# First group of the first FFN: two weight sums moved from VectorE to adding transfers, and the banked functions of every group placed one entry later

## The chip, the cores and the metric

The kernel runs on one core of a Trainium2 chip. The metric is device time in microseconds (us) for one execution, the median of several. Five engines matter here: TensorE (PE, with its weight loads shown as PEld), VectorE (DVE), ScalarE (ACT), GpSimd (POOL) and SyncE (SP). The last two, and ACT now and then, issue the transfers, which run on 16 DMA engines.

## The reference, cut to what matters

The block is one layer of a streaming encoder on 256 frames of 2048 channels, all in float32:

```
x = x + 0.5 * swiglu_ffn(rmsnorm(x, g1), w1_gate, w1_up, w1_down)      # d_ff = 5632
h = rmsnorm(x, gm); proj = h @ w_in                                    # attention, retention, gates
x = x + (sigmoid(gate_a) * branch_a + sigmoid(gate_r) * branch_r) @ w_out
x = x + 0.5 * swiglu_ffn(rmsnorm(x, g2), w2_gate, w2_up, w2_down)
out = rmsnorm(x, gf)
swiglu_ffn(x, wg, wu, wd) = (silu(x @ wg) * (x @ wu)) @ wd
```

The change lies in how `x @ wg` and `x @ wu` are computed in the two FFNs, and in the same machinery for some columns of `w_in`.

## The kernel before, in words

**Entries.** The whole program is one list of entries (`steps`). Each entry multiplies 256 rows of weights by 512 columns. Its `prep` splits the float32 weights into a high and a low part, `hi` by an ACT cast (L136) and `lo` by a DVE subtraction (L137); its `products` are three matmuls for every pair of operands (hi·hi and hi·lo at L147 and L148, lo·hi at L150). A standard entry has 12 matmuls, an entry of a group 6. Four pairs of `hi` and `lo` tiles are in use in turn.

**Order.** `run` walks over the entries. At entry c it first prepares entries up to c+3 (`prep_upto`; fewer at the start), then runs whatever was put off to c with `later(n, fn)`, which means "n entries from here", then issues the products of c. Each engine has its own queue and works through it in program order. So "one entry later" moves an instruction behind the next entry's casts and subtractions in its engine's queue, and POOL, which has little to do, may run far ahead of the others as long as nothing that it waits for is missing.

**Groups.** Two blocks of 512 columns, one of `wu` and one of `wg`, that meet the same operand make a group (`Strassen`): seven products of half the depth stand for eight. A group has 28 entries in four phases. Phase 0 uses the kept weights `k` of four blocks (entries r0 to r3) and their sums `x + k` (entries s0 to s3); phase 1 and phase 2 use freshly loaded weights (r) and further sums (s); phase 3 uses four last sums. The blocks are numbered jc = 0 to 3. Tile names in the profile follow this: in the first group `z10`, `loz1003s` is the low part for phase 0, block 3, entry s, and `z10x`, `z10k` are the two weight tiles of a block.

**First sums.** POOL issues the loads of `k` and `x` for the four blocks (L559, 512 KB each). The first sum x + k is made in one of three ways: by DVE when r of that block is prepared (L548, `first_once`), which is what happens to a block that is not in `group.added`; by an adding transfer `add_on` (L564), which POOL issues `add_wait` = 6 entries behind the load of `x`, for a block in `group.added`; or by DVE later, if nothing did it before. In an FFN the first group has no added blocks, the second has block 0, and all others have blocks 0 and 1 (`ADDED[:n]`, L732). `add_on` waits on POOL's queue until both tiles have landed.

**End of a phase.** `end` moves finished sums of products out of PSUM. Two of the four results of a group are made by DVE from two parts: `c12` (L667) and `c22` (L678), both two entries behind the end of a phase. One entry behind each follows `evict(t, 1, r)`: in an FFN an ACT Silu in place (L801), in the mixing stage an ACT Sigmoid or Silu and a transfer to DRAM (L1090, L1094), for the queries only bookkeeping. A DVE multiplication of `evict(t, 0, ...)` (L804) uses the function's result some entries later.

**Start of the kernel.** `weave` puts ten standard entries (the gate block 10 and the beginning of its partner) ahead of the first group, so that r0 of group `z10` is entry 10; then come r1, a standard entry, s0, r2, s1, r3, a standard entry, s2 and s3, which is entry 19. The first group's eight loads belong to entries 4 to 11, and wait for the third block of the transposed input (`third_block`, L851). In the same stretch ACT makes the squares of the norm (L438), ACT and DVE the sums of the activations (`add_up`, L496 to L510), and POOL the power that gives the norm's scale (L385).

The few lines in which the two edits sit:

```
later(self.add_wait, lambda: add_on(jc))            # in second(), behind the load of x
if jc not in self.added and not self.early:         # in prep of phase 0, entry r
    self.first_once(jc)
later(1, lambda: self.evict(0, 1, r))               # in c12, and likewise in c22
group.added, group.early = group.added[:n], n == 0 and ahead > 8
```

Of the kernel before, what the change touches and what calls it, by code (L numbers as in the profile page):

```python
# [41 lines left out]
RET_WAIT = (14, 5)  # L42
HELD = 6
MIX_ADDED = (0,)
MIX_AHEAD = 12
FIRST_WAIT = 4
HEAD_AT = (3, 6, 10, 13, 17, 20, 24, 27)
# [35 lines left out]
def block_kernel(ctx: ExitStack, tc: tile.TileContext, x, g1, w1g, w1u, w1d, gm, w_in, rel, woa, wor, wo,  # L83
# [21 lines left out]
    def tmp_tile(name, tag="t", bufs=None):  # L105
        return tmp.tile([P, NB], F32, tag=tag, name=name, bufs=bufs)
# [9 lines left out]
    def later(n, fn):  # L116
        due.setdefault(state["step"] + n, []).append(fn)
# [34 lines left out]
    def standard(job, k0):  # L152

        made = {}
        c = len(steps)

        parts = [slice(j, j + 1) for j in range(KC)] if c == 0 else [slice(0, KC)]

        def load():
            made["raw"] = weights_tile(f"raw{c}")  # L160
            fetch(made["raw"], job.w, job.rows[k0], job.col0, parts)

        def prep():
            if c > 0:
                made["hl"] = split(made.pop("raw"), c)
                return

            hi, lo = made["hl"] = split_tiles(c)
            raw = made.pop("raw")
            for p in parts:  # L170
                nc.vector.tensor_copy(hi[:, p, :], raw[:, p, :])
            first_low.extend(lambda p=p: nc.vector.tensor_sub(lo[:, p, :], raw[:, p, :], hi[:, p, :].bitcast(F32)) for p in parts)

        def products(only=None):
            if k0 == 0 and only in (None, 0) and not job.seed:
                open_banks(job)
            hi, lo = made["hl"]
            turns = [
                [
                    (  # L180
                        job.acc[part], job.act(k0 + j, t), (hi[:, j, cs], lo[:, j, cs]),
                        k0 + j == 0 and not job.seed, k0 + j == job.nk - 1,
                    )
                    for j in range(KC)
                ]
                for part, (t, cs) in enumerate(job.parts) if only in (None, part)
            ]

            if 0 < k0 < job.nk - KC:
                turns = [sum(turns, [])]  # L190
            for products in turns:
                three(products, bool(job.seed))
            if only is None and k0 + KC == job.nk:
                close(job)

        return Step(job, k0, load, prep, ("raw",), products)
# [329 lines left out]
    class Strassen:  # L526
# [126 lines left out]
        def end(self, phase, of_sum):  # L653

            norm, acc, wide, name = self.norm, self.acc, self.wide, self.name
            if (phase, of_sum) == (0, False):

                nc.scalar.copy(self.bank("b"), acc["a"])
            elif (phase, of_sum) == (0, True):
                wide["s5"] = tmp_tile(f"{name}s5", "scaled", 1)  # L660
                nc.scalar.activation(wide["s5"], acc["c"], AF.Copy, scale=norm.minus_scale(1))
            elif (phase, of_sum) == (1, True):
                r = tmp_tile(f"{name}c12", "qk", 4)
                nc.scalar.activation(r, acc["a"], AF.Copy, scale=norm.minus_scale(0))

                def c12():
                    nc.vector.scalar_tensor_tensor(r, acc["c"], norm.minus_scale(0), r, op0=ALU.mult, op1=ALU.add)  # L667
                    later(1, lambda: self.evict(0, 1, r))

                later(2, c12)  # L670
            elif (phase, of_sum) == (2, False):
                later(2, lambda: self.evict(0, 0, acc["b"]))
            elif (phase, of_sum) == (2, True):
                r = tmp_tile(f"{name}c22", "qk", 4)
                nc.scalar.activation(r, acc["a"], AF.Copy, scale=norm.minus_scale(1))

                def c22():
                    nc.vector.tensor_add(r, r, wide.pop("s5"))  # L678
                    later(1, lambda: self.evict(1, 1, r))

                later(2, c22)
            elif phase == 3:
                later(1, lambda: self.evict(1, 0, acc["a"]))
# [21 lines left out]
    def weave(jobs, apart, groups, lead, share, start=None, extra=0, ahead=8):  # L705


        queue = [(job, k) for job in jobs for k in range(0, job.nk, KC)]
        at_hand = {}

        def next_standard():

            if len(queue) <= apart:
                return False
            job, k = queue[0]
            if any(at_hand.get(b, len(steps) + 1) > len(steps) for b in job.needs):
                return False
            steps.append(standard(job, k))
            del queue[0]
            if job.makes is not None and k + KC == job.nk:  # L720
                at_hand[job.makes] = len(steps) + 9
            return True

        for _ in range(lead):
            next_standard()
        seconds = []
        rate = (len(queue) - apart) / (len(groups) * sum(share))
        credit = 0.0
        first = max(len(steps) - ahead, D // NB)
        for n, (b, make) in enumerate(groups.items()):  # L730
            group = make()
            group.added, group.early = group.added[:n], n == 0 and ahead > 8  # L732
            loads = group.loads()
            if start is not None and n == 0:
                loads[0] = lambda load=loads[0]: [start(), load()]
            kept.extend((first + i if n == 0 else 0, fn) for i, fn in enumerate(loads))
            for i, part in enumerate(group.steps()):
                if i == HALF_K // KC + 2:
                    seconds.append(len(steps))
                steps.extend(part)  # L740
                credit += rate * share[i]
                if i + 1 == len(share):
                    at_hand[b] = len(steps) + 7

                turn = i + 1 == 3 * (HALF_K // KC)
                if (turn or credit >= (0.2 if (i + 1) % (HALF_K // KC) == 0 else 0.6)) and next_standard():
                    credit -= 1
        if extra:
            due.setdefault(seconds[0], []).append(lambda: room.update(kept=room["kept"] + extra))
            due.setdefault(len(steps), []).append(lambda: room.update(kept=room["kept"] - extra))  # L750
        for job, k in queue:
            steps.append(standard(job, k))

    def ffn(name, norm, wg, wu, wd, after, start=None):
# [83 lines left out]
        for job, follow in zip(jobs, jobs[1:]):  # L838
            job.next = follow
        groups = {b: (lambda b=b: paired(b)) for b in range(nblocks) if b != PLAIN}  # L840
        weave(jobs, len(downs[PASSES[-1]]) * len(PASSES[-1]) * 4 // KC + HELD, groups, LEAD[start is None], SHARE, start, EXTRA)


# [94 lines left out]
    def nat_done(key, b, func, after=None):  # L938
        def done(acc):
            dst = act_tile(F32, f"{key}{b}")  # L940
            nat[key, b] = by_tokens(dst)
            for t in range(NT):
                nc.scalar.activation(nat[key, b][:, t, :], acc[t], func, scale=nm.scale(t))
            if key in to_dram:
                put_away(nat, key, b, dst)
            if after is not None:
                after()

        return done
# [125 lines left out]
    def proj(col, done, tags=("acc", "z")):  # L1075
        return Gemm(w_in0, 0, col, D // P, nm, done, tags)
# [8 lines left out]
    def gates(col1, col2, func, dsts):  # L1085
# [9 lines left out]

        return Strassen(nm, w_in0, col1, w_in0, col2, evict, MIX_ADDED)

# [6 lines left out]
    def queries():  # L1104
# [9 lines left out]

        return Strassen(nm, w_in0, QA, w_in0, QA + NB, evict, MIX_ADDED)

    groups = {"qa": queries, **groups}
    weave(
        [proj(KA + b * NB, att_qk_done("ka", b), both) for b in range(2)]
        + [proj(VA + b * NB, nat_done("va", b, AF.Copy), both) for b in range(2)]  # L1120
        + [proj(VR + b * NB, nat_done("vr", b, AF.Copy), both) for b in range(2)],
        0, groups, MIX_LEAD, MIX_SHARE, None, EXTRA, MIX_AHEAD,
    )
# [212 lines left out]
```

## Time and profile before

| what | value |
|---|---|
| runs | 2047.64, 2048.49, 2049.56 us; median 2048.49 |
| profiled execution, its own time | 2048.31 us |
| its span, first to last instruction | 2046.5 us |
| PE busy | 2031.7 us, 99% of the span |
| DVE busy | 1788.5 us, 87% |
| ACT busy | 1499.2 us, 73% |
| POOL busy | 344.8 us, 17% |
| mean granted TensorE clock | 0.999 of full speed |

The profiled execution took 1.8 us more than its span, and lies 0.18 us under the median. A matmul's recorded duration overlaps that of the next one, so PE's busy share says little about small losses; the distance between the starts of matmuls says more. The share of the other engines is an average over stages that differ.

### The profile page before, as it was taken

To read this page: it belongs to the slowest core of one execution; us is meant where nothing else is said; L and a number is where in the kernel's file an instruction comes from. 1 tells how busy PE (TensorE), PEld (TensorE's weight loads), DVE (VectorE), ACT (ScalarE), POOL (GpSimd) and SP (SyncE) were. 2 spreads that over 40 slices of the span, in tenths; PEclk is the share of its full clock that TensorE was granted. 3 is DMA by queue.
4 is the path that set the end of the run, shared out by engine and by line. 5 is a ranking of instruction groups with operands and counts; after the bars stand their busy time and mean duration, and the time that the engine had idled before them with its cause. 6 is when DMAs were issued, how large, how long until landed. Compare 5 with 4: busy or idle time off the path is not lost.

```text
span 2046.5 us, 26320 instructions
## 1 busy us (share of the span) xinstructions
PE 2031.7 (99%) x9188; PEld 1678.3 (82%) x9188; DVE 1788.5 (87%) x1837; ACT 1499.2 (73%) x1890; POOL 344.8 (17%) x403
## 2 busy tenths in 40 slices
PE   9999999999999999999999999999999999999998
PEld 7788888888888878888888888888788888888886
DVE  7999999999998799999987667569989999989996
ACT  7788887878887777777775434556788788888785
POOL 1221122212113021211120000011112221112200
PEclk9999999999999999999999999999999999999999
DMA  8888899988878689899896645576889988889973
GB/s 289 249 248 259 254 269 278 265 242 246 264 231 264 234 228 310 272 281 286 254 321 221 212 148 197 187 240 180 269 262 269 278 248 234 267 257 268 278 206 134
DMA packets 226853, 506.33 MB, mean 247 GB/s; under 512 B 15824, under 2 KB 16576, under 8 KB 226720
## 3 DMA queue, kind: packets, MB, share of 16 engines
q1 hardware_dynamic: 154560, 297.31, 43.1%
q0 software_dynamic: 67952, 198.36, 37.1%
q10 hardware_dynamic: 4208, 8.99, 1.2%
q8 instruction: 72, 1.18, 0.2%
q14 instruction: 61, 0.50, 0.1%
HBM read 472.08 MB, written 12.06 MB: 237 GB/s over the span
## 4 chain that ended last, share of the span: by engine, by line
PE 94%; DVE 2%; DMA 2%; issue 1%; ACT 0%; POOL 0%; DVEq 0%; POOLq 0%; ACTq 0%
PE acc L150 15%; PE acc L147 15%; PE acc L148 15%; DMA z1030k<-in_ffn_w_up_dram 1%; DMA z1030x<-z1030k 1%; DVE lo L137 0%; DMA raw<-in_ffn_w_gate_dram 0%; PE z704a L150 0%; PE z425a L147 0%; PE z922a L147 0%; PE z885a L148 0%; PE z226a L147 0%; PE z190a L147 0%; PE z46a L147 0%; PE z262a L148 0%
## 5 line engine op out<-in xcount | busy, mean ns | idle before, releaser
L137 DVE TENSOR_TENSOR lo<-raw,hi 128x1024 fp32r<-128x1024 f32 x351 | 428.6, 1223 | 117.7 <-ACT hi L136 116.1
L136 ACT CAST hi<-raw 128x1024 fp32r<-128x1024 f32 x351 | 367.9, 1051 | 178.7 <-PE acc L148 133.4
L824 ACT ACTIVATE xall<-acc 128x512 f32<-128x512 f32 x160 | 94.5, 590 | 13.5 <-PE acc L150 9.7
L821 ACT ACTIVATE acc<-xall 128x512 f32<-128x512 f32 x160 | 95.9, 600 | 2.5
L147 PE MATMUL acc<-hi,mgh 128*128 128x512 f32 x128 | 50.2, 392 | 0.0
L148 PE MATMUL acc<-hi,mgl 128*128 128x512 f32 x128 | 49.8, 389 | 0.0
L150 PE MATMUL acc<-lo,mgh 128*128 128x512 f32 x128 | 35.5, 389 | 0.0
L147 PE MATMUL acc<-hi,nma01h 128*128 128x512 f32 x80 | 32.5, 407 | 0.0
L147 PE MATMUL acc<-hi,nma00h 128*128 128x512 f32 x80 | 32.3, 404 | 0.0
L148 PE MATMUL acc<-hi,nma01l 128*128 128x512 f32 x80 | 31.3, 391 | 0.0
L148 PE MATMUL acc<-hi,nma00l 128*128 128x512 f32 x80 | 31.2, 390 | 0.0
L148 PE MATMUL acc<-hi,nma11l 128*128 128x512 f32 x80 | 31.2, 390 | 0.0
L147 PE MATMUL acc<-hi,nma11h 128*128 128x512 f32 x80 | 31.2, 390 | 0.0
L147 PE MATMUL acc<-hi,nma10h 128*128 128x512 f32 x80 | 31.2, 390 | 0.0
L148 PE MATMUL acc<-hi,nma10l 128*128 128x512 f32 x80 | 31.2, 390 | 0.0
L150 PEld LDWEIGHTS acc<-lo,mgh 128*128 128x128 f32 x128 | 24.0, 188 | 5.0
L148 PEld LDWEIGHTS acc<-hi,mgl 128*128 128x128 f32 x128 | 24.0, 188 | 4.9
L147 PEld LDWEIGHTS acc<-hi,mgh 128*128 128x128 f32 x128 | 24.0, 188 | 4.9
L147 PE MATMUL acc<-hi,atth 128*128 128x512 f32 x64 | 26.2, 410 | 0.0
L147 PE MATMUL acc<-hi,reth 128*128 128x512 f32 x64 | 25.3, 395 | 0.0
L148 PE MATMUL acc<-hi,attl 128*128 128x512 f32 x64 | 25.1, 392 | 0.0
L148 PE MATMUL acc<-hi,retl 128*128 128x512 f32 x64 | 24.9, 389 | 0.0
(6884 smaller groups left out, 7265.9 us busy)
## 6 DMA issues: line engine op xcount, KB each, us to landing
raw<-in_ffn_w_down_dram SPq DMA_DIRECT2D x176, 512.0 KB, 6.8
raw<-in_w_in_dram SPq DMA_DIRECT2D x80, 512.0 KB, 5.2
raw<-in_w_out_dram SPq DMA_DIRECT2D x32, 512.0 KB, 3.7
raw<-in_ffn_w_up_dram SPq DMA_DIRECT2D x16, 512.0 KB, 4.6
raw<-in_w_out_att_dram SPq DMA_DIRECT2D x16, 512.0 KB, 4.2
raw<-in_w_out_ret_dram SPq DMA_DIRECT2D x16, 512.0 KB, 3.8
raw<-in_ffn_w_gate_dram SPq DMA_DIRECT2D x15, 512.0 KB, 4.0
z390x<-in_w_in_dram POOLq DMA_DIRECT2D x8, 512.0 KB, 9.9
```

The costliest lines, as they stand in the source:

```text
L136: nc.scalar.copy(hi, raw)
L137: nc.vector.tensor_sub(lo, raw, hi.bitcast(F32))
L147: nc.tensor.matmul(acc, ahi, whi, start=first, stop=False, **more)
L148: nc.tensor.matmul(acc, alo, whi, start=False, stop=False, **more)
L150: nc.tensor.matmul(acc, ahi, wlo, start=False, stop=last, **more)
L821: nc.scalar.activation(acc, xs[t][:, cols], AF.Copy, scale=2.0)
L824: nc.scalar.activation(xs[t][:, cols], acc, AF.Copy, scale=0.5)
```

## The change

In the first FFN alone, the first group's blocks 2 and 3 get their first sum by an adding transfer, issued two entries behind the load of `x`. In all groups of both FFNs and of the mixing stage, the function of a summed bank comes two entries behind the sum, where it came one entry behind.

```
+FIRST_ADDED = (2, 3)
...
                 def c12():
                     nc.vector.scalar_tensor_tensor(r, acc["c"], norm.minus_scale(0), r, op0=ALU.mult, op1=ALU.add)
-                    later(1, lambda: self.evict(0, 1, r))
+                    later(2, lambda: self.evict(0, 1, r))
...
                 def c22():
                     nc.vector.tensor_add(r, r, wide.pop("s5"))
-                    later(1, lambda: self.evict(1, 1, r))
+                    later(2, lambda: self.evict(1, 1, r))
...
             group = make()
-            group.added, group.early = group.added[:n], n == 0 and ahead > 8
+            group.added = FIRST_ADDED if n == 0 and start is not None else group.added[:n]
+            if n == 0 and start is not None:
+                group.add_wait = 2
+            group.early = n == 0 and ahead > 8
```

`start` is given for the first FFN only.

## The prediction

> **What bounds the kernel now.** I read the page's busy times first, then the windows of the first stretches, then PE's waits there, then the chain.
>
> ```profile
> span 2046.5 us, 26320 instructions
> PE 2031.7 (99%) x9188; PEld 1678.3 (82%) x9188; DVE 1788.5 (87%) x1837; ACT 1499.2 (73%) x1890; POOL 344.8 (17%) x403
> ```
>
> PE is the bound of the kernel as a whole, so a change on DVE or ACT can only win where PE stands still. The windows tell where DVE is as full as PE:
>
> ```profile
> 20.00:40.00 20.00, 19.79 (x91) 16.10 (x90) 16.24 (x19) 16.32 (x28) 6.26 (x9) 1.00 1.01 364
> 40.00:60.00 20.00, 19.15 (x84) 15.32 (x83) 19.97 (x26) 17.35 (x30) 1.09 (x1) 1.00 0.31 93
> 60.00:80.00 20.00, 19.39 (x85) 15.37 (x84) 20.00 (x19) 14.04 (x16) 4.78 (x6) 1.00 0.88 241
> 80.00:100.00 20.00, 19.43 (x86) 14.74 (x86) 19.50 (x21) 14.57 (x19) 8.40 (x11) 1.00 1.04 301
> 100.00:120.00 20.00, 20.00 (x94) 16.66 (x93) 18.27 (x18) 16.82 (x23) 0.93 (x1) 1.00 0.83 275
> ```
>
> After the length come PE, PEld, DVE, ACT and POOL. From 40 to 100 us DVE is full (19.97, 20.00, 19.50 of 20) and PE is not; from 100 us on PE is full and DVE has room. What PE waits for between 40 and 106 us is this, and it is all DVE's:
>
> ```profile
> PE z10c L150 <- DVE loz1003s L137: 0.9, 1, 0.9
> PE acc L150 <- DVE lo L137: 0.6, 1, 0.6
> PE z10b L150 <- DVE loz1023r L137: 0.5, 1, 0.5
> ```
>
> The chain of that stretch, followed back from 106 us, says the same in order of time:
>
> ```profile
> 46.11 0.97 DVE loz1001s L137
> ...
> 49.42 1.14 DVE z10x L548
> ...
> 73.74 1.15 DVE lo L137
> ...
> 74.93 0.73 PE acc L150 x2
> ...
> 88.27 1.14 DVE loz1023r L137
> ...
> 89.44 0.44 ACT hiz1022s L136
> ...
> 89.90 1.24 DVE loz1022s L137
> ...
> 91.18 0.74 PE z10a L150 x2
> ```
>
> From 46 to 75 us the chain is on DVE without a break, and one of the two sums that the change takes away stands in it. How much PE loses is seen from the starts of its matmuls:
>
> ```profile
> 45.90 0.39 PE L147 MATMUL z10a<-hiz1002r,n1a00h 128*128 128x512 f32 x1
> 75.50 0.39 PE L147 MATMUL acc<-hi,n1a11h 128*128 128x512 f32 x1
> 93.15 0.39 PE L147 MATMUL acc<-hi,f1a10h 128*128 128x512 f32 x1
> 104.03 0.39 PE L147 MATMUL z46a<-hiz4600r,n1a00h 128*128 128x512 f32 x1
> 106.75 0.39 PE L147 MATMUL acc<-hi,f1a10h 128*128 128x512 f32 x1
> ```
>
> Between the last two lie two entries of six matmuls: 2.72 us, 0.2267 us each, the pace without waits. Between the first two lie eleven entries of the group with 66 matmuls and four and a half standard ones with 54, 120 in all, so 27.20 us at that pace, and they took 29.60: PE loses 2.40 us there. From 75.50 to 93.15 lie half a standard entry and ten of the group, 66 matmuls or 14.96 us, and eight transposes:
>
> ```profile
> 110.84 1.03 PE L394 MATMUL f1a0p<-id_sb,z10c 128*128 128x128 f32 x8
> 111.63 0.48 PE L147 MATMUL z46a<-hiz4602r,n1a00h 128*128 128x512 f32 x1
> ```
>
> Eight of them without a wait take 0.79 us, so 15.75 us of the 17.65 are work and 1.90 are lost. All that the start of the first group can give back is 2.40 + 1.90 = 4.30 us, 0.21% of the kernel. What a measurement of this kernel can tell from no change is about 0.2%, or 4.1 us.
>
> **The two sums.** Each DVE sum that goes occupies DVE's queue for 1.14 us (the chain's row at 49.42), so DVE's queue is shorter by 1.14 us from block 2's sum on and by 2.28 us from block 3's on, since in 40 to 80 us DVE is never idle for long. An earlier DVE helps only if its inputs are there. The two casts on ACT that read the sums, the wait that goes with the second, and the subtraction on DVE behind it:
>
> ```profile
> 48.66 1.05 ACT L136 CAST hiz1002s<-z10x 128x1024 fp32r<-128x1024 f32 x1
> 50.65 1.05 ACT L136 CAST hiz1003s<-z10x 128x1024 fp32r<-128x1024 f32 x1 [0.33 <-DVE z10x L548]
> ...
> 54.82 1.22 DVE L137 TENSOR_TENSOR loz1003s<-z10x,hiz1003s 128x1024 fp32r<-128x1024 f32 x1
> ```
>
> With DVE 2.28 us ahead, `loz1003s` would start at about 52.5, and its cast ends at 51.7 or, without the 0.33 us of waiting, at 51.4: the input is there. So the low part is ready at 53.8, where PE has waited for it from 55.1 (0.9 us up to its end at 56.0): that wait is gone. Followed through, ACT moves up too where it waited for DVE or PE, and I find no DVE subtraction up to `loz1023r` whose cast would then be late by more than a tenth. The second loss, at 74.93, is cut by DVE's 2.28 us as long as PE can use them, and PE's own limit is the 2.40 us above. I take 2.28.
>
> What is late next: the adding transfers themselves. POOL's queue, the landing of the loads of `x` for blocks 2 and 3 (issued at 24.08 and 25.52), and the transfers of this kind that the trace shows:
>
> ```profile
> 24.08 0.74 POOL L559 DMA_DIRECT2D z10x<-in_ffn_w_gate_dram  x1
> ...
> 25.52 0.74 POOL L559 DMA_DIRECT2D z10x<-in_ffn_w_gate_dram  x1
> 53.80 1.09 POOL L385 TENSOR_TENSOR n1rstd<-v,mhalf 128x2 f32<-128x2 f32 x1 [27.54 <-DVE v L384]
> ```
>
> ```profile
> z10x<-in_ffn_w_gate_dram POOLq DMA_DIRECT2D x1, 512.0 KB, 13.0
> ```
>
> ```profile
> z10x<-in_ffn_w_gate_dram POOLq DMA_DIRECT2D x1, 512.0 KB, 15.5
> ```
>
> ```profile
> DMA to landing us min/median/max: 4.6/6.7/12.2
> ```
>
> The loads land at 37.1 and 41.0 us. POOL waits for each in its queue, and behind the two added issues stands nothing until the power at 53.80, so the wait blocks no one: two issues of at most about 1 us fit twelve times over. The adding transfers took 4.6 to 12.2 us from issue to landing, 6.7 in the middle, mostly beside full DMA engines. Block 3's then lands between 45.6 and 53.2 us, by the middle value at 47.7, and is wanted by ACT at about 50.3. After the loads the DMA engines stand idle:
>
> ```profile
> 44.00:50.00 6.00, 6.00 (x28) 4.85 (x27) 6.00 (x8) 6.00 (x12) 0.00 (x0) 1.00 0.00 0
> ```
>
> With a share of 0.00 between 44 and 50 us the low end is nearer than the high one; I take 46 to 48 and count the transfers at nothing. At the high end ACT would stand 2.9 us at `hiz1003s`, and the casts for the next standard entry and for phase 1 are queued behind it, with DVE and in the end PE waiting for those.
>
> The windows show the DMA engines full (1.01) from 20 to 40 us, where block 2's transfer would be issued. The Trainium skill, "DMA: Bandwidth & Descriptors", section "Issuing engines are not separate DMA queues", says that transfers started by different engines run on the same 16 DMA engines and interleave. That speaks against an extra transfer in such a stretch: by that rule its half megabyte at 364 GB/s, an estimate of 1.4 us, is taken from the loads behind it, block 3's among them, and the late transfer below gets likelier and dearer by 1.4 us, while the sum would stay.
>
> **The functions one entry later.** In the queue of ACT the first group shows what a function directly behind its sum costs:
>
> ```profile
> 88.31 0.63 ACT L801 ACTIVATE z10c<-z10c 128x512 f32<-128x512 f32 x1 [3.51 <-DVE z10c L667]
> ```
>
> ACT stands 3.51 us for a sum that DVE reaches late, and the casts `hiz1022s` and `hiz1023s` are behind it; DVE then waits 0.50 us for the first of them (89.40 to 89.90; the chain has the cast in it) and PE waits on that. One entry later the cast goes first. I count 0.50 us, on top of the 2.28. The second FFN's first group has the same pair of waits, and again DVE has a hole of 0.50 us ahead of a stretch in which PE waits:
>
> ```profile
> PE f2a0p L394 <- DVE z704c L804: 0.7, 1, 0.7
> ```
>
> ```profile
> 1442.96 1.23 DVE L137 TENSOR_TENSOR loz74001r<-z740k,hiz74001r 128x1024 fp32r<-128x1024 f32 x1 [0.50 <-ACT hiz74001r L136]
> ```
>
> That gives 0.50 us more, between nothing (if a load holds DVE up right behind it) and 0.50. In the other groups ACT's wait is 1 us or less, and PE shows no loss to recover: nothing. The price of being later is on DVE's multiplication (L804), which needs the function. In a steady group the two are far apart:
>
> ```profile
> 163.43 0.63 ACT L801 ACTIVATE z46c<-z46c 128x512 f32<-128x512 f32 x1 [0.94 <-DVE z46c L678]
> ...
> 168.44 0.75 DVE L804 SCALAR_TENSOR_TENSOR z46c<-z46a,n1rstd,z46c 128x512 f32<-128x512 f32 x1
> ```
>
> From the function's end at 164.06 to the multiplication at 168.44 lie 4.4 us; an entry of the group is 1.36 us of matmuls and a standard one 2.72, so the function still ends in time. In the mixing stage the transfer to DRAM goes one entry later too, and is read back much later.
>
> **Sum.** 2.28 + 0.50 + 0.50 = 3.28 us less. The profiled execution, 2048.31 us, would take 2045.0; against the median of the runs, 2048.49, that is 2045.2, my forecast.
>
> **Rivals.** *The lead is not handed on.* ACT is nearly as full as DVE from 44 to 50 us (6.00 of 6.00), and if its casts become the bound, only the first wait of 0.9 us goes: 2047.6. For it speaks that row; against it ACT's share of 14.04 of 20 us from 60 to 80, and its 3.51 us wait.
>
> *All the lost time comes back.* If PE also gets rid of its many small delays, the 4.30 us at the start go whole, and with them the second FFN's 0.7 us, 5.0 in all: 2043.5. Against it: DVE stays full, and a queue shorter by 2.28 us can give no more than that until ACT's hole adds to it.
>
> *A late transfer makes it slower.* The place is ACT's cast `hiz1003s`. Up to a landing at 52.6 us, the stall is less than the lead of 2.28 us; beyond it DVE is later than before. At 12.2 us from issue to landing, the top of the row, the landing is at 53.2 and ACT's queue loses 2.9 us: 0.6 us slower, 2049.1, with the 1.4 us of the skill's rule 2050.5. For it: transfers behind full DMA engines took that long. Against it: the idle DMA engines from 44 us.
>
> *It does nothing there*, if block 2's and 3's sums stay on DVE. The adding is issued in entries 11 and 13 and the sums are first used in 15 and 16, so the flag is set by then; 2048.5 with a chance of 0.02.
>
> **How the numbers follow.** The forecast has 0.63, the lead not handed on 0.16, all coming back 0.12, the late transfer 0.07, nothing 0.02. The range goes from 2043.2, the third case's 2043.5 and 0.3 us for the scatter of a median of runs that lie 1.9 us apart, to 2048.4, which takes in the second and leaves out about half of the first rival's spread above no change and the slower case. Faster by over 0.2% means under 2044.4: the third case and 0.07 of the forecast's spread, 0.19. Slower by over 0.2% needs the transfer later than any row shows, or some cost that I do not see: 0.05. The rest, 0.76, is within 0.2%.
>
> **What would show it.** Right: two L548 sums of `z10x` instead of four, two L564 issues at about 37 to 42 us, landings before 50 us, no PE wait for `loz1003s`, at 93 us PE ahead by 2.8 us, no ACT wait of 3.5 us at L801. Wrong: an ACT wait at `hiz1002s` or `hiz1003s` for the transfer; PE waits at 75 or 88 us as long as before; a DVE wait for L801 at L804; or a difference that arises after 120 us, outside the second FFN's start.

## The result and the profile after

Over 20 runs each, the kernel before took 2048.14 us in the median (2047.09 to 2050.23) and the changed one 2045.26 us (2044.06 to 2047.15). The ratio is 0.9984, with a 95% interval of 0.9978 to 0.999, so 0.16% less, 0.10 to 0.22%; the two medians themselves lie 2.88 us apart, 0.14%. The forecast was 3.28 us less, and 2045.2 us.

Line numbers of the changed kernel are one higher up to L732 and four higher behind it (L137 is L138, L548 is L549, L801 is L805). What PE waits for between 40 and 106 us, three rows before, is one row after:

```profile
PE z10b L151 <- DVE loz1023r L138: 0.5, 1, 0.5
```

The windows of the same stretches (length, then PE, PEld, DVE, ACT, POOL with their counts, the granted clock, the DMA engines' share, GB/s):

```profile
40.00:60.00 20.00, 20.00 (x90) 16.57 (x89) 19.97 (x26) 18.54 (x32) 2.11 (x3) 1.00 0.68 181
60.00:80.00 20.00, 20.00 (x89) 15.87 (x88) 20.00 (x19) 15.01 (x17) 6.45 (x8) 1.00 0.89 239
80.00:100.00 20.00, 19.52 (x88) 15.74 (x87) 20.00 (x21) 15.91 (x20) 6.70 (x9) 1.00 1.05 321
```

PE is full from 40 to 80 us, where it had 19.15 and 19.39 of 20. DVE is no less full than before; it does the same list with two items struck out, and so is further along from those two items on. The clearest measure for what follows is the stretch of the first group, from its first matmul to the second group's. Before, it ran from 39.10 to 104.03, 64.93 us; after, by PE's timeline:

```profile
39.66 0.39 PE L148 MATMUL z10a<-hiz1000r,n1a00h 128*128 128x512 f32 x1
...
101.93 0.39 PE L148 MATMUL z46a<-hiz4600r,n1a00h 128*128 128x512 f32 x1
```

That is 62.27 us, 2.66 less, against a whole profiled execution that went from 2048.31 to 2045.62 us, 2.69 less. That the two agree so closely is in part chance: this trace starts the first group 0.56 us later than the one before, and takes 0.49 us less between the second group and the second FFN's first. A second trace of the changed kernel took 2.61 us less in the stretch and 3.16 less in all (2045.15 us).

The added transfers, from POOL's timeline, and the time to landing of each:

```profile
39.21 0.94 POOL L565 DMA_DIRECT2D z10x<-z10k  x1 [12.39 <-DMA z10x<-in_ffn_w_gate_dram]
43.28 0.86 POOL L565 DMA_DIRECT2D z10x<-z10k  x1 [3.13 <-DMA z10x<-in_ffn_w_gate_dram]
52.07 1.10 POOL L386 TENSOR_TENSOR n1rstd<-v,mhalf 128x2 f32<-128x2 f32 x1 [7.93 <-DVE v L385]
```

```profile
z10x<-z10k POOLq DMA_DIRECT2D x1, 512.0 KB, 6.9
```

```profile
z10x<-z10k POOLq DMA_DIRECT2D x1, 512.0 KB, 7.1
```

POOL stands for the loads, 12.39 and 3.13 us, as predicted, and nothing waits behind it. The sums are there at 46.1 and 50.4 us. ACT's and DVE's rows where they are used:

```profile
49.21 1.05 ACT L137 CAST hiz1002s<-z10x 128x1024 fp32r<-128x1024 f32 x1
50.79 1.04 ACT L137 CAST hiz1003s<-z10x 128x1024 fp32r<-128x1024 f32 x1
```

```profile
53.10 1.22 DVE L138 TENSOR_TENSOR loz1003s<-z10x,hiz1003s 128x1024 fp32r<-128x1024 f32 x1
```

No wait stands at the two casts, but block 3's sum is only 0.4 us early in this trace. In four more traces in which block 3's sum is made by a transfer in the same place it is 1.8 to 3.2 us early (2.1 in the second trace of the change: issued at 41.79, landed 6.5 us later, cast at 50.40). The subtraction starts 13.44 us behind the group's first matmul, where it started 15.72 behind it: 2.28 us sooner, two sums' worth to the hundredth. The function behind its sum:

```profile
83.21 1.06 ACT L137 CAST hiz1022s<-z10k 128x1024 fp32r<-128x1024 f32 x1
86.58 0.63 ACT L805 ACTIVATE z10c<-z10c 128x512 f32<-128x512 f32 x1 [2.31 <-DVE z10c L668]
```

The cast now goes ahead of the function. ACT still stands 2.31 us at the function, but what DVE needs next has been cast by then.

### The profile page after: what moved, and what is told of

It reads as the page before. It is cut to its first block, busy times and chain, and to the rows that moved or that the text cites. A ratio compares the mean times of both kernels' runs of the same rounds, so it can differ in the third digit from the quotient of the medians.

```text
span 2043.8 us, 26275 instructions
## 1 busy us (share of the span) xinstructions
PE 2031.2 (99%) x9188; PEld 1679.2 (82%) x9188; DVE 1787.5 (87%) x1835; ACT 1504.3 (74%) x1890; POOL 346.6 (17%) x405
## 4 chain that ended last, share of the span: by engine, by line
PE 98%; DVE 1%; issue 0%; DMA 0%; ACT 0%; POOL 0%; DVEq 0%; POOLq 0%; ACTq 0%
PE acc L151 15%; PE acc L148 15%; PE acc L149 15%; DMA raw<-in_ffn_w_gate_dram 0%; PE z390a L151 0%; PE z1030a L151 0%; PE z425a L149 0%; PE z885a L148 0%; PE z190a L148 0%; PE z118a L148 0%; PE z958a L148 0%; PE z777a L149 0%; PE z334a L149 0%; PE z82a L149 0%; PE z994a L151 0%
## 5 line engine op out<-in xcount | busy, mean ns | idle before, releaser
L138 DVE TENSOR_TENSOR lo<-raw,hi 128x1024 fp32r<-128x1024 f32 x351 | 427.5, 1220 | 119.8 <-ACT hi L137 117.0
L137 ACT CAST hi<-raw 128x1024 fp32r<-128x1024 f32 x351 | 367.8, 1050 | 184.6 <-PE acc L149 137.9
```

The lines of the kernel that those rows point to most:

```text
L137: nc.scalar.copy(hi, raw)
L138: nc.vector.tensor_sub(lo, raw, hi.bitcast(F32))
```

## The experiments

Each kernel is the changed one with the edit shown, unless it says otherwise; the functions alone are the kernel before with one edit, so their rows have the old line numbers. Behind the change, the ratios were formed against other runs of the kernel before, taken on the same occasion (medians 2048.13 and 2048.87 us), not against the 2048.14 of the first row. The stretch of the first group and the times of all of them:

| kernel | first group's stretch, us | median, us | ratio to the kernel before, 95% interval |
|---|---|---|---|
| before | 64.93 | 2048.14 | |
| both edits (the change) | 62.27, again 62.32 | 2045.26 | 0.9984 [0.9978, 0.999] |
| the sums alone | 62.64 | 2046.14 | 0.999 [0.9981, 0.9999] |
| the functions alone | 64.58, again 64.54 | 2047.85 | 0.9996 [0.9987, 1.0005] |
| two sums left out | 62.32 | 2045.27 | 0.9987 [0.9978, 0.9996] |
| three sums by transfer | 64.20 | 2047.49 | 0.9994 [0.9985, 1.0003] |
| late transfer | 68.82 | 2051.96 | 1.0015 [1.0006, 1.0024] |
| DVE's sum c12 later | 62.04 | 2044.69 | 0.9984 [0.9976, 0.9993] |
| block 2 alone | 63.40 | one run, 2047.25 | |
| block 3 alone | 63.44 | one run, 2044.97 | |

The stretch is the difference of two starts on PE's timeline, one trace each; the two kernels that were traced twice agree with themselves within 0.05 us, so differences of a few tenths can be read, which the times, with intervals of 1.2 to 1.8 us to either side, do not allow.

**The sums alone, and the functions alone.** The first kernel is the changed one with the functions put back to one entry; the second is the kernel before with the functions put off to two, and so leaves the sums on DVE.

```
-                    later(2, lambda: self.evict(0, 1, r))      # the sums alone, against the changed kernel; likewise evict(1, 1, r)
+                    later(1, lambda: self.evict(0, 1, r))
...
-                    later(1, lambda: self.evict(0, 1, r))      # the functions alone, against the kernel before; likewise evict(1, 1, r)
+                    later(2, lambda: self.evict(0, 1, r))
```

> The first edit alone: blocks 2 and 3 of the first group by adding transfers, the functions one entry behind their sum as before. Measured on the stretch from the first matmul of the first group to that of the second: 64.93 us before, 62.27 with both edits. Theory (DVE's queue shorter by 2.28 us, and ACT's stand at the function worth 0.4 to 0.5 us on its own): about 62.7 us, so 2.2 us less than before, the ACT wait of about 3.5 us at the function still there, and the second FFN's second group's stretch at 65.5 us as before; time about 2.3 us under the kernel before. Rival (the lead is handed on only because ACT no longer stands): 64.0 us, 0.9 less.

> The second edit alone: all four first sums of the first group on DVE, the functions two entries behind their sum. Theory: the first group's stretch about 64.4 us (0.5 less than before), the second FFN's second group's about 65.15 (0.36 less), time about 0.9 us less, within what the times can tell. Rival (DVE has no use for an earlier cast while it carries the two sums): 64.9 us and no difference there. Rival (the functions are what frees PE): about 62.5 us.

The sums alone give 2.29 us in the stretch (64.93 to 62.64), the functions alone 0.35, and the two together 2.66: they add up. PE's starts show where each arises. At phase 1, block 2, entry s, the kernel before is 37.77 us behind its group's first matmul and the sums alone 35.51 us, 2.26 less, and that lead is kept up to the second group:

```profile
76.87 0.39 PE L147 MATMUL z10a<-hiz1012s,n1s6h 128*128 128x512 f32 x1
```

```profile
39.16 0.39 PE L148 MATMUL z10a<-hiz1000r,n1a00h 128*128 128x512 f32 x1
74.67 0.39 PE L148 MATMUL z10a<-hiz1012s,n1s6h 128*128 128x512 f32 x1
101.80 0.39 PE L148 MATMUL z46a<-hiz4600r,n1a00h 128*128 128x512 f32 x1
```

With the functions alone PE is level with the kernel before up to `hiz1022s`, whose low part is the one that DVE starts 0.50 us late in the kernel before, and 0.33 us ahead at the next entry of the group, `hiz1023s`. In the kernel with the sums alone the old stand and DVE's hole are still there, only earlier:

```profile
86.09 0.63 ACT L805 ACTIVATE z10c<-z10c 128x512 f32<-128x512 f32 x1 [3.49 <-DVE z10c L668]
```

```profile
85.97 1.23 DVE L138 TENSOR_TENSOR loz1023r<-rawz1023r,hiz1023r 128x1024 fp32r<-128x1024 f32 x1
87.69 1.23 DVE L138 TENSOR_TENSOR loz1022s<-z10k,hiz1022s 128x1024 fp32r<-128x1024 f32 x1 [0.50 <-ACT hiz1022s L137]
```

and in the kernel with the functions alone the hole is closed, at the old place:

```profile
88.06 1.21 DVE L137 TENSOR_TENSOR loz1023r<-rawz1023r,hiz1023r 128x1024 fp32r<-128x1024 f32 x1
89.19 1.21 DVE L137 TENSOR_TENSOR loz1022s<-z10k,hiz1022s 128x1024 fp32r<-128x1024 f32 x1
```

The rivals of both fall. The expectation of 65.15 us for the second FFN's second group (from its first matmul to the third group's) does not hold for the functions alone (65.81); more on that below.

**One sum at a time.**

```
-FIRST_ADDED = (2, 3)
+FIRST_ADDED = (2,)        # and (3,) in the other kernel
```

> Both edits, but only block 2's first sum by adding transfer; block 3's is back on DVE. Theory (each sum taken from DVE is worth its 1.14 us in the queue, as long as PE is waiting for DVE): first group's stretch 63.4 us, half way between the second edit alone (64.56, mean of two) and both edits (62.30). Rival (the PE wait for block 3's low part is what counts, and either sum's removal clears it): 62.6 to 63.0 us.

> Both edits, but only block 3's first sum by adding transfer; block 2's is back on DVE. Theory: first group's stretch 63.4 us, as with block 2 alone, since both sums stand ahead of the low part for which PE waits first. Rival (one sum clears the first wait, and the later waits follow other rules): 62.6 to 63.0 us.

```profile
39.11 0.39 PE L148 MATMUL z10a<-hiz1000r,n1a00h 128*128 128x512 f32 x1
102.51 0.39 PE L148 MATMUL z46a<-hiz4600r,n1a00h 128*128 128x512 f32 x1
```

```profile
39.23 0.39 PE L148 MATMUL z10a<-hiz1000r,n1a00h 128*128 128x512 f32 x1
102.67 0.39 PE L148 MATMUL z46a<-hiz4600r,n1a00h 128*128 128x512 f32 x1
```

63.40 and 63.44 us: each sum taken off DVE is worth its own 1.14 us, whichever it is. The first group is bound by the length of DVE's queue and not by one particular wait.

**The two sums left out.** This kernel does not add blocks 2 and 3 at all, so part of the computation is missing.

```
-                group.add_wait = 2
+                group.summed.update(FIRST_ADDED)
```

> Both edits, but the first sums of blocks 2 and 3 of the first group are left out altogether, neither on DVE nor by transfer. Shows what the two transfers cost where they lie. Theory (nothing: the second lands 0.4 us before ACT asks for it): first group's stretch 62.2 to 62.4 us, as with the transfers. Rival (the transfers delay loads or casts): at least 0.4 us shorter, 61.9 or less.

62.32 us, and the changed kernel's two traces have 62.27 and 62.32. So the two transfers cost nothing where they lie. The windows of the changed kernel show that this is not because they are small:

```profile
44.00:46.00 2.00, 2.00 (x10) 1.66 (x9) 2.00 (x4) 2.00 (x5) 0.14 (x1) 1.00 1.04 312
46.00:48.00 2.00, 2.00 (x10) 1.68 (x9) 2.00 (x4) 2.00 (x5) 0.00 (x0) 1.00 1.03 222
```

They fill the 16 DMA engines in a stretch in which, without them, nothing moves; in the kernel without the sums the same two windows read:

```profile
44.00:46.00 2.00, 2.00 (x11) 1.65 (x10) 2.00 (x4) 2.00 (x4) 0.00 (x0) 1.00 0.03 9
46.00:48.00 2.00, 2.00 (x11) 1.65 (x10) 2.00 (x4) 2.00 (x5) 0.00 (x0) 1.00 0.00 0
```

**A third sum.**

```
-FIRST_ADDED = (2, 3)
+FIRST_ADDED = (1, 2, 3)
...
-                    later(self.add_wait, lambda: add_on(jc))
+                    later(4 if self.add_wait == 2 and jc == 1 else self.add_wait, lambda: add_on(jc))
```

> Both edits, and block 1's first sum by adding transfer too, issued behind all eight loads and ahead of the other two. DVE's queue is shorter by another 1.14 us. Theory (the margin of 0.4 us is used up: two transfers kept the DMA engines full for six us, so a third puts the last landing about 3 us later, to 53 or 54, and block 1's own landing at about 44 to 46 against 43.5 when ACT asks): ACT waits 2 to 3 us in all for transfers and the stretch is 62.3 to 64.0 us, no better than with two. Rival (landing keeps pace): down to 61.2 us.

64.20 us, a little worse than the range that I gave. Block 1's transfer is issued at 34.53, while the loads still fill the DMA engines, takes 10.8 us, and comes too late:

```profile
45.37 1.05 ACT L137 CAST hiz1001s<-z10x 128x1024 fp32r<-128x1024 f32 x1 [2.03 <-DMA z10x<-z10k]
```

```profile
46.45 1.23 DVE L138 TENSOR_TENSOR loz1001s<-z10x,hiz1001s 128x1024 fp32r<-128x1024 f32 x1 [1.78 <-ACT hiz1001s L137]
```

DVE has holes of 0.58 us ahead of ACT's stand, where without the third sum it runs ahead of the cast `hiz1002r`, and of 1.78 and 0.27 us behind it. That is 2.63 us, more than the 1.14 us that the third sum saves. Block 3's transfer was not late: issued at 42.65, it landed 9.2 us later at 51.9, and ACT, by then late itself, asked at 52.7. That part of the expectation was wrong.

**A late transfer.** Block 3's transfer goes into entry 15 and behind a POOL multiplication.

```
+                    if self.add_wait == 2 and jc == 3:
+                        behind = small.tile([P, 1], F32, tag="behind", name="behind", bufs=1)
+                        nc.gpsimd.tensor_tensor(behind, self.norm.ssum[:, 0, 3:4], mhalf[:, :1], op=ALU.mult)
                     nc.gpsimd.dma_start(self.x[jc], self.kept[jc], accum_op=ALU.add)
...
-                    later(self.add_wait, lambda: add_on(jc))
+                    later(4 if self.add_wait == 2 and jc == 3 else self.add_wait, lambda: add_on(jc))
```

> Both edits, and block 3's adding transfer made late: it is put into entry 15 and behind a small POOL multiplication that reads one of the norm's sums of squares, which ACT finishes about 48.5 us into the run. So it is issued at about 49.5 instead of 43.3 and lands, beside idle DMA engines, at 54.5 to 56.5, where ACT asks for it at 50.8. Theory of the prediction (ACT stands at that cast, everything behind it moves, and from a landing of about 53 us on, in this run's time, the first group is later than before): ACT waits 4 to 5.5 us there, the first group's stretch becomes 66 to 67.5 us (64.93 before, 62.27 with both edits), time 1 to 2.5 us over the kernel before. Rival (DVE and PE have enough work at hand for the wait to be covered): 62.3 to 63 us.

It came later than meant. The multiplication stood behind the norm's power on POOL's queue, so the transfer was issued at 52.73 us and landed 4.6 us later:

```profile
57.38 1.04 ACT L137 CAST hiz1003s<-z10x 128x1024 fp32r<-128x1024 f32 x1 [7.07 <-DMA z10x<-z10k]
```

The direction is that of the theory: the kernel is slower than before, by 0.15% (0.06 to 0.24%), and the work at hand covers only part of the wait. The size comes near the theory's as well: it gave 66 to 67.5 us for a wait of 4 to 5.5, so some 69.1 for 7.07, and 68.82 was measured. But that is two errors against each other. PE stood for 4.4 us of ACT's 7.07, so some 2.7 us were covered; and the windows show a loss that the theory did not have, in the third value from the end, the granted clock:

```profile
54.00:56.00 2.00, 0.22 (x1) 0.00 (x0) 0.00 (x0) 0.00 (x0) 0.00 (x0) 1.00 1.03 197
56.00:58.00 2.00, 0.00 (x0) 0.00 (x0) 0.00 (x0) 0.62 (x1) 0.00 (x0) 0.59 0.35 66
58.00:60.00 2.00, 1.52 (x4) 1.24 (x5) 1.39 (x3) 2.00 (x4) 0.00 (x0) 0.50 0.00 0
60.00:62.00 2.00, 2.00 (x6) 1.58 (x5) 1.76 (x2) 2.00 (x3) 0.00 (x0) 0.50 0.00 0
62.00:64.00 2.00, 2.00 (x8) 1.58 (x7) 2.00 (x3) 1.82 (x3) 0.00 (x0) 0.71 0.76 223
64.00:66.00 2.00, 2.00 (x10) 1.66 (x9) 2.00 (x3) 1.06 (x1) 0.00 (x0) 1.00 0.59 132
```

PE stands for 4.4 us, and then its clock is granted at 0.59, 0.50, 0.50 and 0.71 in the next four windows: matmuls start 0.43 us apart where 0.2267 is the pace. Added up over PE's starts, the excess is 4.42 us for the stand and about 2.3 us for the slow matmuls behind it; the stretch is 6.55 us longer than with both edits. The Trainium skill, "TensorE: Matmul & The Clock Gate", section "Part 1: The HAM clock gate (the "warmup" mystery)", says that the clock falls to half after an idle window of about 3.4 us; the trace agrees as to the level, with 0.50 in a stand of 4.4 us. As to the time it does not: the clock is at 1.00 up to 56.2 us and at 0.50 from 56.4 on, about 2.1 us after the end of PE's last matmul at 54.2, so it fell sooner than after 3.4 us of idleness.

**DVE's sum one entry later.** A try at the one wait that is left.

```
-                later(2, c12)
+                later(3, c12)
```

> Both edits, and in all groups DVE's first sum of a finished bank (c12) three entries behind the end of its phase instead of two, its function still two behind it. Aims at the one PE wait of 0.5 us that is left in the first group, for a subtraction that stands in DVE's queue right behind that sum (0.66 us). Theory: that wait goes and the first group's stretch is 61.6 to 61.9 us, 0.4 to 0.7 less than with both edits; the time 0.5 less, too little for the times to tell. Rival (the sum delays the next subtraction instead): 62.2 to 62.3 us.

The PE wait for `loz1023r` is gone, and no PE wait at all is listed from 36 to 110 us. But the stretch is 62.04, only 0.26 us less than the 62.30 of both edits: part of the loss moved to the next subtraction. By PE's starts, counted from the group's first, this kernel is 0.65 us ahead of the change at `hiz1022s` and 0.25 at `hiz1023s`. Neither expectation holds, theory and rival each have a part. At 2044.69 us this kernel has the lowest median of all, with the same ratio to its own runs of before (0.9984) as the change; that it is faster than the change is not shown.

**The same kernels again.**

> The changed kernel once more, unaltered, to see how far its trace repeats. First group's stretch 62.2 to 62.4 us if that stretch is fixed by the queues; the second FFN's second group's stretch, 65.15 us, again below 65.3 if the second edit is what shortened it, anywhere from 65.0 to 65.8 if it hangs on when its loads land.

> The second edit alone once more, unaltered. First group's stretch 64.5 to 64.7 us as in its first run (64.58); the second FFN's second group's stretch, 65.81 us in the first run, again 65.7 or more if the edit lengthens it there, anywhere from 65.0 to 65.8 if it hangs on when its loads land.

The first group repeats within 0.05 us. The second FFN's second group does not: 65.15 and 65.03 us for both edits, 65.81 and 64.54 for the functions alone, 65.51 before, 65.35 for the sums alone. One piece of code varies by more than the effect that I looked for.

## Why the prediction was right, point by point

- **PE is the bound, and can only gain where it waits for DVE, from 46 to 92 us.** Right: the first group's stretch is 2.66 us shorter, and the sums alone and the functions alone gain at the places named. At 93 us PE is 2.66 us ahead, counted from the group's start, where 2.8 was named.
- **The two sums are worth 2.28 us.** Right, and the best supported point: 2.29 us for the sums alone, 1.16 and 1.12 for either one (from 64.56, the mean of the functions alone, to 63.40 and 63.44), and the subtraction for block 3 starts 2.28 us sooner within its group.
- **The transfers cost nothing.** Right in the sum, with a margin that differs from trace to trace. I took 46 to 48 us for block 3's landing, from a middle of 6.7 us and idle DMA engines. In the first trace it landed at 50.4: the load came at 42.7 and not at 41.0, the transfer took 7.1 us, and the two transfers themselves kept the engines full. ACT asked 0.4 us later. In the second trace it landed at 48.3, 2.1 us before ACT asked.
- **More transfers delay the loads behind them.** The rule that I weighed in the prediction (the Trainium skill, "DMA: Bandwidth & Descriptors", section "Issuing engines are not separate DMA queues") gave an estimate of 1.4 us for block 3's load. Its landing took 15.5 us before, 16.6 and 15.5 in the two traces with both edits, and 16.0 where the transfers were left out, so these runs do not show it either way.
- **The function one entry later is worth 0.50 us in the first group.** Right in kind, a little less in size: 0.35 and 0.39 us alone (two traces) and 0.34 on top of the sums (62.64 to 62.30). DVE's hole of 0.50 us is closed in both kernels that have the edit.
- **And 0.50 us in the second FFN's first groups.** This is the term that failed. DVE's hole at `loz74001r` is gone with the edit, but what PE loses there varies from run to run by more than 0.50 us, and nothing that repeats came out of it. The sum counted DVE's hole as PE's gain there, and the runs do not bear that out: for the first two groups together the functions alone gave 127.04 and 125.52 us in two traces of one kernel, against 126.49 before. Where ACT waits long for one weight load, the first two groups together take longer with that wait; here are the waits between 1420 and 1450 us of the kernel with block 2 alone and of the second run of the functions alone, one of the longest and the shortest in the first two groups together:

```profile
ACT hi L137 <- DMA raw<-in_ffn_w_up_dram: 3.9, 1, 3.9
```

```profile
ACT hi L136 <- DMA raw<-in_ffn_w_up_dram: 1.4, 1, 1.4
```

  Together the groups take 62.19 + 65.76 and 60.98 + 64.54 us. Over the nine traces with a wait of 1.4 us or more the time of the two rises with it (125.5 at 1.4, 126.0 at 1.9, 127.0 at 2.9, 128.2 at 4.1). That is not the whole account: before, and in the first trace of both edits, ACT has no wait for that load there, and the two groups take 126.49 and 126.13. The two kernels with one sum each, alike in the first group to 0.04 us, differ by 2.3 us in the first two groups of the second FFN (127.95 against 60.94 + 64.71), which is all of the 2.28 us between their times. That the load's landing is the cause was not tested, and what moves it stays open.
- **In the other groups nothing.** Not shown either way. From the second group to the second FFN's first, some 1278 us, the twelve traces lie between 1277.2 and 1278.6, so a gain of a few tenths cannot be read there.
- **The signs named.** One sign of being wrong did appear, and the prediction held all the same: PE's wait at 88 us, for `loz1023r`, is 0.5 us as before. It comes later in DVE's queue than the place where the two sums are saved, right behind DVE's sum c12, and PE arrives at it as much earlier as DVE does. It was a bad sign to choose. And "no ACT wait of 3.5 us" says nothing of the sums: with the sums alone ACT still waits 3.49 us, and the 2.29 us are there.
- **The rivals.** "The lead is not handed on" fell with the sums alone. "All the lost time comes back" did not happen: `loz1023r` still costs PE 0.5 us. "A late transfer makes it slower" is real as a mechanism; the margin to it at ACT's cast was 0.4 us in one trace of the change and 2.1 in the other. Its price was 0.9 us too high, what is left of two errors against each other. By its rule, ACT's wait less the lead of 2.28, the 7.07 us of the late transfer are 4.8 us over the kernel before, and the stretch measured 3.9 over it. The rule let all of ACT's wait reach PE, where 4.4 of 7.07 us did, and had no term for the clock, which cost 2.3. Where it breaks even was not measured.

Without the second FFN's term the sum is 2.78 us. The first group measured 2.66 and 2.61, and the medians lie 2.88 apart. The sum of 3.28 was too high by that one term, which is a fifth of the width of the interval of the times (2.5 us). That the forecast of 2045.2 us was met to within 0.1 us is luck: the difference was 0.4 us too large, and the median of three runs from which it was taken, 2048.49, was 0.35 us above the median of twenty.

## What to carry to other kernels

When the bound engine waits for another one that is full over a whole stretch, count the items taken off that other engine's queue: here each was worth its own length in the queue, whichever it was, until the next limit was reached. Work moved to a transfer was free where the result landed before it was asked for, though the transfers filled the DMA engines; the first two sums met that by 0.4 us or more, and the third missed it by 2. Take that margin from more than one trace: it changed by 1.7 us between two of the same kernel. An operation that waits for another engine does its harm through what is queued behind it, so place it behind the next thing that somebody needs.

## What the runs showed of the hardware

- An adding transfer of 512 KB within SBUF took 4.6 us from issue to landing with the DMA engines to itself (late transfer) and 5.0 to 10.8 us in the first group beside others. One alone filled the engines at 197 GB/s (1.03, late transfer), and the windows with two of them show 1.03 to 1.04 at 222 to 312 GB/s; before the change, loads from DRAM filled them at 364 GB/s.
- In a PE stand of 4.4 us the granted clock fell to 0.50 and stayed there for some 6.8 us in all, an estimate from the four windows (0.59, 0.50, 0.50, 0.71). The slow matmuls cost 2.3 us, half as much again as the stand.
- Two traces of one kernel agree to 0.05 us over 62 us of a stretch that DVE bounds, and differ by 1.3 us over 65 us of a stretch of the second FFN, in which ACT's wait for a load also differs (2.9 and 1.4 us).
